# One VectorE instruction per modulation block, and a planner's time line with traced durations, in a two-part transformer forward pass

## The chip, the cores and the metric

One NeuronCore of a Trainium2 chip runs one program. The metric is the device time of one launch in microseconds (us); lower is better. All operands live in HBM before the launch and the result is written back to HBM.

## What is computed

The reference chains two small transformers over 512 tokens of width 1024, all in float32. The first has two layers, each a hybrid mixer (window attention, dense attention, spatial gating), a cross attention and a convolutional feed-forward network. The second has an even layer (a state-space mixer beside differential attention), an odd layer (retention beside sliding-window attention) and an MLP after each. Every sublayer of the second part is wrapped in a modulation that depends on one vector `c` alone:

```
c_act = jax.nn.silu(c)
...
def sandwich(x, c_act, sublayer, g_pre, g_post, w_mod, b_mod):
    shift, scale, gate = jnp.split(c_act @ w_mod + b_mod, 3, axis=-1)
    h = rms_norm_2(x, g_pre) * (1 + scale[:, None]) + shift[:, None]
    return x + gate[:, None] * rms_norm_2(sublayer(h), g_post)
```

There are four such sublayers, so `c_act @ w_mod` is four products of a vector of 1024 with a matrix of 1024 by 3072. In the kernel it is 96 blocks of 128 rows by 1024 columns: 8 blocks (one per 128 rows of `w_mod`) sum to one of 12 results.

## The kernel before

**Products.** A float32 product is made of three TensorE products of `fp32r` halves: a weight block of 128x1024 arrives by DMA as `raw`, ScalarE writes its high half `whi`, VectorE the rest `wlo` (`split_block`, line 489), and `mm3` (line 501) issues hi*hi, hi*lo and lo*hi. Activations are kept transposed as `fTh`/`fTl`. There are 531 such blocks. Names in the trace: `bank` is a PSUM tile, `W`-like names are weight halves, `gh`/`gl` the halves of a feed-forward activation.

**Order of the work.** Nothing is scheduled by the compiler. The Python program keeps a *time line* (`Line`, line 194): for every instruction that it emits, `add` works out when the engine and the operands would be free, with a duration from `cost` (line 262). Work that is to come later is put on a heap by `defer` (line 345), with a due time from that time line (when its operands are ready), and `poll` (line 332) emits what is due after every few TensorE instructions. `pump` (line 459) splits weight blocks ahead while VectorE's time on the line is at most 1 us past TensorE's. So the numbers in `cost` decide in which order each in-order engine gets its instructions; the chip waits on semaphores where reality is later than the line. Every recorded instruction has the source line 186 (the recorder).

**The modulation** is done inside the two convolutional feed-forward stages, 48 blocks in each. `mod_step` (line 1282) is called after each feature product; `mod_go` (line 1289) handles one block `mraw` once its DMA is due on the line. The first of 8 blocks is scaled into the accumulator `macc` by ScalarE; each of the other 7 is scaled in place by ScalarE and added by GpSimd (POOL). After the eighth, `sums` is deferred: four TensorE products with a matrix of ones add up the 128 rows of `macc`.

**Other places.** `hybrid` (line 871) loads the gate bias `bg` and halves it on VectorE as the first thing of a layer. `launch` (line 851) starts the 16 attention units of a branch, whose `probs_out` (line 765) writes the tiles `pt0`, `pt1`. `diff` runs eight heads that share one buffer `qkl`.

Of the kernel before, what the change touches and what calls it, by code (L numbers as in the profile page):

```python
# [13 lines left out]
F32R = mybir.dt.float32r  # L14
# [8 lines left out]
NT = S // P  # L23
# [170 lines left out]
class Line:  # L194
# [66 lines left out]
    @staticmethod  # L261
    def cost(eng, op, n, ins, outs):
        if op == "dma_start":
            return 1.03 if eng == "gpsimd" else 0.05
        if eng == "tensor":
            if op == "transpose":
                return 0.107
            fast, m = ins[0].dtype == F32R, ins[0].shape[1]
            if m > 64:
                return max(n / 2400 + 0.003, 0.108 if n > 64 else 0.2) if fast else max(n / 600 + 0.005, 0.22)  # L270
            return max(n, 64) / (2400 if fast else 600) * (0.56 if m > 32 else 0.29)
        if eng == "vector":
            if op == "tensor_scalar_mul":
                return 0.06 + n / 1530
            return (0.13 if op == "scalar_tensor_tensor" else 0.07) + n / 960
        if eng == "scalar":
            return 0.03 + n / 1120 + 0.08 * max(0, len(ins) + len(outs) - 2)
        return 0.07 + n / 460 if n > 64 else 0.62


class Block:
# [22 lines left out]
class KB:  # L304
# [460 lines left out]
    def probs_out(self, pool, u):  # L765


        nc, sh = self.nc, u.shared
        if not sh:
            sh["pt"] = [self.tile(pool, (P, u.wide // P, 2, P), f"pt{e}") for e in range(2)]  # L770
            sh["ev"] = Event(2, lambda: self.defer(0, pv, *sh["pt"]))
        for e in range(2):
            pp = self.ps((P, 4, P))
            self.transpose4(pp, [u.sc[e][:, b * P:b * P + P] for b in range(u.nkb)])
            pt = sh["pt"][e][:, :u.nkb, u.pr, :]
            if e == 0:
                nc.scalar.activation(pt, pp[:, :u.nkb, :], AF.Copy)
            else:
                nc.vector.tensor_copy(pt, pp[:, :u.nkb, :])
        u.read.set()  # L780

        def pv():
            po = self.ps((P, 2 * P))
            vc = slice(64 * u.kv, 64 * u.kv + 64)
            for b in range(u.nkb):
                for e in range(2):
                    nc.tensor.matmul(po[64 * e:64 * e + 64, :], lhsT=u.v[:, u.b0 + b, vc],
                                     rhs=sh["pt"][e][:, b, :, :].rearrange("p r q -> p (r q)"),
                                     start=b == 0, stop=b == u.nkb - 1)
            self.poll()  # L790
            sl, k = slice(u.i * P, u.i * P + P), 2 * u.kv
            self.split(u.br.h[:, k:k + 2, sl], u.br.l[:, k:k + 2, sl], po.rearrange("p (r q) -> p r q", r=2))

        sh["ev"].set()

# [55 lines left out]
    def launch(self, pool, unit, step, br, **kw):  # L851


        units, depth = [], kw["bufs"] // 2

        def start(n):
            if n >= depth and not units[n - depth].read.done:
                units[n - depth].read.after(lambda: self.defer(0, lambda: start(n)))
                return
            unit(pool, units[n])  # L860

        for n in range(16):
            kv, i, pr = n // 8, n // 2 % 4, n % 2
            u = Unit(kv=kv, i=i, pr=pr, shared={} if pr == 0 else units[-1].shared, br=br, read=Event(),
                     **{k: v for k, v in kw.items() if k != "band"})
            u.b0, u.nkb, u.add = kw["band"](i)
            units.append(u)
            self.defer(n * step, lambda n=n: start(n), kw["kh"], kw["kl"])


    def hybrid(self, l, xT):
        nc, A = self.nc, self.A
        with self.pool("hp") as hp:
            W = Weights(self, "w_in", l)
            WB = Weights(self, "w_branch", l)
            bg = self.load(hp, A["b_gate"][l], (P, 24), "bg")
            nc.vector.tensor_scalar_mul(bg, bg, 0.5)
            mg = self.tile(hp, (P, KD, S), "mg")

            def branch(n, br, first, done=None):  # L880
                wb = None
                for m in range(KD):
                    c = n * 8 + m
                    ps = self.dense(W.next(), 0, xT, KD)
                    gt = self.tile(hp, (P, S), "gt", 2)
                    nc.scalar.activation(gt, ps, AF.Tanh, bias=bg[:, c:c + 1], scale=0.5)
                    if m % 2 == 0:
                        wb = WB.next()
                    ps = self.dense(wb, (m % 2) * P, br, 4, keep=m % 2 == 0)
                    if first:  # L890
                        nc.vector.scalar_tensor_tensor(mg[:, m, :], gt, 1.0, ps, op0=ALU.add, op1=ALU.mult)
                    else:
                        nc.vector.scalar_tensor_tensor(gt, gt, 1.0, ps, op0=ALU.add, op1=ALU.mult)
                        nc.vector.tensor_tensor(mg[:, m, :], mg[:, m, :], gt, op=ALU.add)
                    if done:
                        done(m)

            def new_br():
                return FT(*self.pair(hp, (P, 4, S), "br", 2))

            brc = new_br()
            with self.pool("cp") as cp:
                self.branch_c(cp, l, xT, W, brc)
                self.flush()
            bra = new_br()
            with self.pool("ap") as ap, ExitStack() as es:
                self.branch_ab(es, ap, l, xT, W, bra, "a")
                branch(2, brc, True)
                self.flush()
            brb = new_br()  # L910
            with self.pool("ap") as ap, ExitStack() as es:
                self.branch_ab(es, ap, l, xT, W, brb, "b")
                branch(0, bra, False)
                self.flush()
            with self.pool("mt") as mt:
                hi, lo = self.pair(mt, (P, KD, S), "mT")
                mT = FT(hi, lo, (), [Event() for _ in range(KD)])

                def merged(m):
                    def go():  # L920
                        self.split(hi[:, m, :], lo[:, m, :], mg[:, m, :], scale=0.5)
                        mT.ev_k[m].set()
                    self.defer(0, go, mg[:, m, :])

                branch(1, brb, False, merged)
                self.flush_to_k(mT)
                self.open_boundary(self.open_right(), A["ln1_g"], A["ln1_b"], l)
                WM = Weights(self, "w_mix_out", l)
                fT, after = self.ln_start()
                self.tok(WM, mT, KD, 512, lambda t, ps: self.residual(t, 0, ps), by_k=True)  # L930
                self.tok(WM, mT, KD, 512, lambda t, ps: (self.residual(t, 1, ps), after(t)))
        return fT
# [356 lines left out]
    def mod_go(self):  # L1289
# [9 lines left out]
        if k == 0:  # L1299
            self.mod_acc = self.tile(self.mod_pool, (P, D), "macc", 2)  # L1300
            nc.scalar.activation(self.mod_acc, raw, AF.Copy, scale=ck)
        else:
            nc.scalar.activation(raw, raw, AF.Copy, scale=ck)
            nc.gpsimd.tensor_tensor(self.mod_acc, self.mod_acc, raw, op=ALU.add)
        if k == KD - 1:
            acc, row = self.mod_acc, self.mod_sums[kind][s]

# [428 lines left out]
    def diff(self, dp, hT, W, v, yT):  # L1736
        nc, A = self.nc, self.A
        sub = self.load(dp, A["e_diff_norm"], (P, 1), "sub")
        nc.vector.tensor_scalar_mul(sub, sub, 1.0 - LAM_INIT)

        def head(h):
            T = self.tile(dp, (P, 512), "T", 2)
            self.toeplitz(T, h, 0, 512)
            qk = []
            shared = {}

            def unit(i):
# [3 lines left out]
                for m in range(2):  # L1751
                    ps = self.ps()
                    self.scores(ps[:, :Wd], qk[0][:, m, i * P:i * P + P], qk[1][:, m, :Wd], qk[2][:, m, :Wd], Wd)
                    s = self.tile(dp, (P, Wd), f"sc{i}", 2)
                    nc.vector.tensor_tensor_reduce(s, ps[:, :Wd], T[:, 384 - i * P:512], 1.0, NEG,
                                                   ALU.add, ALU.max, mx[:, m:m + 1])
                    s2.append(s)
                nc.vector.tensor_scalar_mul(nm_, mx, -1.0)
                for m in range(2):
                    nc.scalar.activation(s2[m], s2[m], AF.Exp, bias=nm_[:, m:m + 1], accum_out=sums[:, m:m + 1])  # L1760
# [49 lines left out]
            def ev(i, ps):  # L1810
                t = self.tile(dp, (P, 2, S), f"qk{i}", 2, F32R)
                qk.append(t)
                if i == 0:
                    self.stack_q([t[:, e, :] for e in range(2)], ps, HD ** -0.5)
                else:
                    qk.append(self.tile(dp, (P, 2, S), "qkl", 1, F32R))
                    self.stack_k(t, qk[2], ps)
                    for n in range(NT):
# [295 lines left out]
```

## Time and profile before

| | |
|---|---|
| median of 3 runs | 3478.86 us (3476.7 to 3480.21) |
| the profiled execution's own time | 3478.01 us |
| its span, first to last instruction | 3476.2 us |
| mean granted TensorE clock | 0.987 |
| busy: TensorE / VectorE / ScalarE / GpSimd | 3366.9 / 2078.5 / 1433.7 / 347.3 us |

The span is 1.8 us less than the execution's own time. A busy time is the sum of the stretches in which an engine had an instruction in it. Where TensorE is not busy, a view of waits names the engine whose result it waited for.

### The profile page before, as it was taken

To read this page: it belongs to the slowest core of one execution; us is meant where nothing else is said; L and a number is where in the kernel's file an instruction comes from. 1 tells how busy PE (TensorE), PEld (TensorE's weight loads), DVE (VectorE), ACT (ScalarE), POOL (GpSimd) and SP (SyncE) were. 2 spreads that over 40 slices of the span, in tenths; PEclk is the share of its full clock that TensorE was granted. 3 is DMA by queue.
4 is the path that set the end of the run, shared out by engine and by line. 5 is a ranking of instruction groups with operands and counts; after the bars stand their busy time and mean duration, and the time that the engine had idled before them with its cause. 6 is when DMAs were issued, how large, how long until landed. Compare 5 with 4: busy or idle time off the path is not lost. (4 is left out here: it accounts for less than half of the span.)

```text
span 3476.2 us, 42309 instructions
## 1 busy us (share of the span) xinstructions
PE 3366.9 (97%) x16500; PEld 2749.0 (79%) x16500; DVE 2078.5 (60%) x3370; ACT 1433.7 (41%) x2497; POOL 347.3 (10%) x250
## 2 busy tenths in 40 slices
PE   8999999999999999999999899999999999999999
PEld 6887887777778878887777678777888887888887
DVE  5767467665667674676656666487433466553334
ACT  3544334544335452444543343475332344433222
POOL 0010001432200100013322000001000010010000
PEclk9999999999999999999999999999999999999999
DMA  4221445644332224445443221313322331333222
GB/s 147 70 69 60 143 155 181 207 164 145 118 118 70 72 67 140 158 177 182 162 153 118 86 79 55 100 49 136 104 97 97 121 111 55 103 138 109 93 95 87
DMA packets 116760, 399.24 MB, mean 115 GB/s; under 512 B 14608, under 2 KB 18592, under 8 KB 116560
## 3 DMA queue, kind: packets, MB, share of 16 engines
q1 hardware_dynamic: 115984, 394.44, 33.4%
q8 instruction: 130, 2.13, 0.2%
q0 software_dynamic: 576, 2.10, 0.2%
q14 instruction: 70, 0.57, 0.1%
HBM read 375.39 MB, written 23.71 MB: 115 GB/s over the span
## 5 line engine op out<-in xcount | busy, mean ns | idle before, releaser
L186 DVE TENSOR_TENSOR wlo<-raw,whi 128x1024 fp32r<-128x1024 f32 x531 | 716.5, 1354 | 688.5 <-ACT whi L186 678.4
L186 PE MATMUL bank<-fTh,whi 128*128 128x512 f32 (+1 forms) x2320 | 886.8, 382 | 0.0
L186 PE MATMUL bank<-fTl,whi 128*128 128x512 f32 (+1 forms) x2320 | 872.4, 376 | 0.4
L186 PE MATMUL bank<-fTh,wlo 128*128 128x512 f32 (+1 forms) x2320 | 871.8, 376 | 0.1
L186 ACT ACTIVATE whi<-raw 128x1024 fp32r<-128x1024 f32 x531 | 553.6, 1047 | 379.2 <-PE bank L186 345.8
L186 PEld LDWEIGHTS bank<-fTh,whi 128*128 128x128 f32 x2320 | 441.4, 190 | 90.5 <-issue 10.5
L186 PEld LDWEIGHTS bank<-fTh,wlo 128*128 128x128 f32 x2320 | 441.0, 190 | 85.4 <-DVE wlo L186 0.5
L186 PEld LDWEIGHTS bank<-fTl,whi 128*128 128x128 f32 x2320 | 441.5, 190 | 79.8 <-DVE fTl L186 1.3
L186 PE MATMUL bank<-whi,gh 128*128 128x512 f32 x864 | 343.2, 397 | 0.0
L186 PE MATMUL bank<-whi,gl 128*128 128x512 f32 x864 | 342.5, 396 | 0.0
L186 PE MATMUL bank<-wlo,gh 128*128 128x512 f32 x864 | 342.4, 396 | 0.0
L186 POOL TENSOR_TENSOR macc<-macc,mraw 128x1024 f32<-128x1024 f32 x84 | 225.9, 2690 | 449.2 <-ACT mraw L186 448.0
L186 PE MATMUL bank<-whi,fTh 128*128 128x512 f32 (+2 forms) x608 | 231.5, 381 | 12.8 <-ACT whi L186 7.1
L186 PE MATMUL bank<-wlo,fTh 128*128 128x512 f32 (+2 forms) x608 | 224.1, 369 | 9.9 <-DVE wlo L186 9.9
L186 PE MATMUL bank<-whi,fTl 128*128 128x512 f32 (+2 forms) x608 | 223.7, 368 | 0.5 <-DVE fTl L186 0.5
L186 PEld LDWEIGHTS bank<-whi,gh 128*128 128x128 f32 x864 | 163.1, 189 | 40.1 <-issue 0.8
L186 PEld LDWEIGHTS bank<-wlo,gh 128*128 128x128 f32 x864 | 163.2, 189 | 39.4
L186 PEld LDWEIGHTS bank<-whi,gl 128*128 128x128 f32 x864 | 162.9, 188 | 39.5
L186 POOL TENSOR_TENSOR rstd<-rstdv,mhalf 128x1 f32<-128x1 f32 x68 | 56.5, 832 | 1053.1 <-DVE rstdv L186 1050.5
L186 DVE SCALAR_TENSOR_TENSOR y<-bank,cv,y 128x511 f32<-128x511 f32 x176 | 131.3, 747 | 37.2 <-ACT y L186 34.1
L186 PEld LDWEIGHTS bank<-whi,fTh 128*128 128x128 f32 x608 | 115.9, 191 | 33.7 <-ACT whi L186 8.8
L186 PEld LDWEIGHTS bank<-wlo,fTh 128*128 128x128 f32 x608 | 116.0, 191 | 29.7 <-DVE wlo L186 12.3
(322 smaller groups left out, 4649.4 us busy)
## 6 DMA issues: line engine op xcount, KB each, us to landing
raw<-in_mlp_w_dram SPq DMA_DIRECT2D x128, 512.0 KB, 3.3
mraw<-in_mod_w_dram SPq DMA_DIRECT2D x96, 512.0 KB, 4.7
raw<-in_w_in_dram SPq DMA_DIRECT2D x88, 512.0 KB, 3.3
raw<-in_f_w_up_dram SPq DMA_DIRECT2D x88, 512.0 KB, 4.2
raw<-in_e_w_in_dram SPq DMA_DIRECT2D x48, 512.0 KB, 4.1
raw<-in_f_w_down_dram SPq DMA_DIRECT2D x40, 512.0 KB, 3.5
raw<-in_o_w_in_dram SPq DMA_DIRECT2D x30, 512.0 KB, 4.3
raw<-in_w_branch_dram SPq DMA_DIRECT2D x24, 512.0 KB, 3.3
```

Of the source, the lines that this page charges most:

```text
L186: r = f(*a, **k)
```

## The change

Three things change. The seven additions per result become one `scalar_tensor_tensor` on VectorE each (`macc = mraw * ck + macc`), which replaces both the ScalarE scaling and the GpSimd addition. The durations in `cost` get other constants. And three ordering details are new: an attention unit's `probs_out` waits until the products of the pair of units before it have been emitted, a `diff` head writes its key halves only after the scores of the head before, and the halving of `bg` stands behind branch c.

```diff
@@ cost
-            fast, m = ins[0].dtype == F32R, ins[0].shape[1]
+            m = ins[0].shape[1]
+            if ins[0].dtype == F32R:
+                return max(n / 2270 + 0.007, 0.112)
             if m > 64:
-                return max(n / 2400 + 0.003, 0.108 if n > 64 else 0.2) if fast else max(n / 600 + 0.005, 0.22)
-            return max(n, 64) / (2400 if fast else 600) * (0.56 if m > 32 else 0.29)
+                return max(n / 600 + 0.005, 0.22)
+            return max(n, 64) / 600 * (0.56 if m > 32 else 0.29)
         if eng == "vector":
             if op == "tensor_scalar_mul":
-                return 0.06 + n / 1530
-            return (0.13 if op == "scalar_tensor_tensor" else 0.07) + n / 960
+                return 0.15 + n / 1530
+            return (0.21 if op == "scalar_tensor_tensor" else 0.155) + n / 960
         if eng == "scalar":
-            return 0.03 + n / 1120 + 0.08 * max(0, len(ins) + len(outs) - 2)
-        return 0.07 + n / 460 if n > 64 else 0.62
+            acc = len(outs) > 1
+            return 0.145 + n / 1128 + (0.19 if acc else 0.0) + 0.09 * max(0, len(ins) + len(outs) - 2 - acc)
+        return 0.07 + n / 460 if n > 64 else 0.6
@@ probs_out
+        if not u.before.done:
+            u.before.after(lambda: self.defer(0, lambda: self.probs_out(pool, u)))
+            return
...
             self.split(u.br.h[:, k:k + 2, sl], u.br.l[:, k:k + 2, sl], po.rearrange("p (r q) -> p r q", r=2))
+            u.over.set()
@@ launch
+            u.before, u.over = (units[-1].before, units[-1].over) if pr else (units[-1].over if units else Event(0), Event())
@@ hybrid
-            nc.vector.tensor_scalar_mul(bg, bg, 0.5)
...
                 self.branch_c(cp, l, xT, W, brc)
+                nc.vector.tensor_scalar_mul(bg, bg, 0.5)
@@ mod_go
-            nc.scalar.activation(raw, raw, AF.Copy, scale=ck)
-            nc.gpsimd.tensor_tensor(self.mod_acc, self.mod_acc, raw, op=ALU.add)
+            nc.vector.scalar_tensor_tensor(self.mod_acc, raw, ck, self.mod_acc, op0=ALU.mult, op1=ALU.add)
@@ diff
+        scored = [Event(0)]
         def head(h):
+            before, now = scored[-1], Event(NT)
+            scored.append(now)
...
+                now.set()
...
+                    self.wait(before)
                     qk.append(self.tile(dp, (P, 2, S), "qkl", 1, F32R))
```

The new constants reorder all engines. Two places matter below. First, VectorE at the start of the program, from the memset of `ones` on (`fTl` is the low half of the transposed input, `bg` the gate bias). Before:

```order
L186 MEMSET ones 128x128
L186 TENSOR_SCALAR bg_114<-bg_114 128x24
L186 TENSOR_TENSOR fTl_93<-bank_25_133,fTh_92 128x4x128
L186 TENSOR_TENSOR fTl_93<-bank_26_140,fTh_92 128x4x128
L186 TENSOR_TENSOR wlo_148<-raw_99,whi_147 128x1024
L186 TENSOR_TENSOR fTl_93<-bank_30_156,fTh_92 128x4x128
```

Now:

```order
L186 MEMSET ones 128x128
L186 TENSOR_TENSOR fTl_93<-bank_25_132,fTh_92 128x4x128
L186 TENSOR_TENSOR fTl_93<-bank_26_139,fTh_92 128x4x128
L186 TENSOR_TENSOR wlo_147<-raw_99,whi_146 128x1024
L186 TENSOR_TENSOR fTl_93<-bank_30_155,fTh_92 128x4x128
L186 TENSOR_TENSOR fTl_93<-bank_31_162,fTh_92 128x4x128
```

The row that reads `bg` no longer stands ahead of the first input halves; it comes after branch c.

Second, TensorE around the second sum of the modulation in the first feed-forward stage (`macc` with `ones`). Before:

```order
L186 MATMUL bank_1159_5890<-fTh_4854,whi_5746 128x512
L186 MATMUL bank_1159_5890<-fTl_4855,whi_5746 128x512
L186 MATMUL bank_1159_5890<-fTh_4854,wlo_5747 128x512
L186 MATMUL bank_1165_5922<-macc_5632,ones 32x256 x4
L186 MATMUL bank_1159_5890<-fTh_4854,whi_5746 128x512
```

Now:

```order
L186 MATMUL bank_1159_5900<-whi_5855,gh_5362 128x512
L186 MATMUL bank_1159_5900<-wlo_5856,gh_5362 128x512
L186 MATMUL bank_1159_5900<-whi_5855,gl_5363 128x512
L186 MATMUL bank_1164_5917<-macc_5616,ones 32x256 x4
L186 MATMUL bank_1160_5901<-whi_5855,gh_5362 128x512
```

The sum has moved from within the last feature product of the group to nine products behind its end. On VectorE the last addition of that sum now stands here, between two splits and the two convolution steps of the last feature product:

```order
L186 TENSOR_TENSOR wlo_5856<-raw_5725,whi_5855 128x1024
L186 SCALAR_TENSOR_TENSOR macc_5616<-mraw_5791,cact,macc_5616 128x1024
L186 SCALAR_TENSOR_TENSOR y_1156_5894<-bank_1152_5861,cv_5075,y_1156_5894 128x511 x2
L186 TENSOR_TENSOR wlo_5903<-raw_5776,whi_5902 128x1024
L186 TENSOR_TENSOR y_1156_5894<-y_1148_5850,y_1156_5894 128x512
```

The two convolution steps behind the addition read the bank of the last feature product, so the addition stands ahead of work that needs that product's end, and the sum on TensorE behind it.

## Rows read from the trace of the kernel before

**Rows 1.** The page: busy time of each engine, share of the span, instructions

```profile
PE 3366.9 (97%) x16500; PEld 2749.0 (79%) x16500; DVE 2078.5 (60%) x3370; ACT 1433.7 (41%) x2497; POOL 347.3 (10%) x250
```

**Rows 2.** TensorE's waits: releaser, us in total, times, longest

```profile
PE bank L186 <- POOL macc L186: 36.5, 12, 5.1
PE bank L186 <- DVE ss L186: 14.1, 3, 4.8
PE bank L186 <- DVE wlo L186: 9.9, 5, 6.1
PE bank L186 <- ACT whi L186: 7.1, 4, 2.5
...
PE bank L186 <- ACT fTh L186: 5.7, 1, 5.7
...
PE bank L186 <- DVE mx L186: 3.5, 2, 1.9
PE bank L186 <- ACT bank L186: 2.9, 4, 1.3
```

**Rows 3.** Timeline, second sum: start, us, engine, instruction, idle before and releaser

```profile
653.60 2.68 DVE L186 TENSOR_TENSOR wlo<-raw,whi 128x1024 fp32r<-128x1024 f32 x1 [2.75 <-ACT whi L186]
...
660.81 1.13 ACT L186 ACTIVATE mraw<-mraw,cact 128x1024 f32<-128x1024 f32 x1
...
662.09 2.35 POOL L186 TENSOR_TENSOR macc<-macc,mraw 128x1024 f32<-128x1024 f32 x1 [3.53 <-ACT mraw L186]
...
664.49 1.08 PE L186 MATMUL bank<-macc,ones 128*32 128x256 f32 x8 [5.08 <-POOL macc L186]
```

**Rows 4.** Stretches: busy us of PE, PEld, DVE, ACT, POOL; granted clock; DMA

```profile
661.00:664.49 3.49, 0.01 (x1) 0.01 (x1) 2.13 (x3) 1.83 (x3) 2.35 (x1) 0.60 0.82 305
664.49:668.30 3.81, 3.81 (x15) 2.43 (x16) 1.38 (x2) 3.78 (x6) 0.00 (x0) 0.50 0.60 209
...
667.00:668.00 1.00, 1.00 (x4) 0.81 (x3) 1.00 (x1) 0.97 (x3) 0.00 (x0) 0.50 0.11 41
...
669.00:670.00 1.00, 1.00 (x6) 0.77 (x6) 0.60 (x2) 1.00 (x2) 0.92 (x1) 1.00 0.77 209
```

**Rows 5.** Same view: both feed-forward stages, and 50 us of uninterrupted products

```profile
569.00:905.00 336.00, 317.62 (x1434) 254.81 (x1435) 213.44 (x196) 161.38 (x194) 113.09 (x42) 0.97 0.52 179
1517.00:1853.00 336.00, 317.45 (x1431) 255.22 (x1432) 211.54 (x194) 160.84 (x193) 112.85 (x42) 0.97 0.49 172
...
2550.00:2600.00 50.00, 50.00 (x216) 40.25 (x215) 20.24 (x23) 15.13 (x19) 0.00 (x0) 1.00 0.29 97
```

**Rows 6.** Groups by form, 569 to 905 us: busy, mean ns, idle before

```profile
L186 DVE TENSOR_TENSOR wlo<-raw,whi 128x1024 fp32r<-128x1024 f32 x56 | 105.5, 1887 | 68.5 <-ACT whi L186 65.1 <-DMA mraw<-in_mod_w_dram 3.0
L186 DVE TENSOR_TENSOR y<-y,y 128x512 f32<-128x512 f32 x19 | 24.0, 1263 | 0.0
...
L186 ACT ACTIVATE mraw<-mraw,cact 128x1024 f32<-128x1024 f32 x42 | 47.5, 1138 | 0.0
...
L186 POOL TENSOR_TENSOR macc<-macc,mraw 128x1024 f32<-128x1024 f32 x42 | 113.1, 2693 | 224.5 <-ACT mraw L186 223.9
```

**Rows 7.** Groups by form: splits in 50 to 470 us, others in the span

```profile
L186 DVE TENSOR_TENSOR wlo<-raw,whi 128x1024 fp32r<-128x1024 f32 x59 | 71.8, 1222 | 55.0 <-ACT whi L186 52.9 <-PE bank L186 1.8 <-DMA gb<-in_ln_b_dram 0.3
...
L186 DVE TENSOR_TENSOR r<-r 128x512 f32<-128x512 f32 x64 | 43.8, 684 | 0.0
...
L186 DVE SCALAR_TENSOR_TENSOR y<-y,rstd,gb 128x1024 f32<-128x1024 f32 x20 | 25.7, 1285 | 3.8 <-POOL rstd L186 2.2
```

**Rows 8.** Timeline of the first 25 us: ScalarE, VectorE and TensorE

```profile
8.02 1.05 ACT L186 ACTIVATE whi<-raw 128x1024 fp32r<-128x1024 f32 x1
9.12 0.80 PE L186 MATMUL bank<-whi,fTh 128*128 128x512 f32 x1 [1.63 <-ACT whi L186]
13.44 0.18 DVE L186 TENSOR_SCALAR bg<-bg 128x24 f32<-128x24 f32 x1 [10.32 <-DMA bg<-in_b_gate_dram]
16.00 0.80 PE L186 MATMUL bank<-wlo,fTh 128*128 128x512 f32 x1 [6.08 <-DVE wlo L186]
```

## Prediction

> **What bounds the kernel now.** I begin with the table of busy times: TensorE is busy for 97% of the span, 3366.9 us, with VectorE at 60% [rows 1]. So the time is TensorE's products, plus its idle time of 3476.2 - 3366.9 = 109.3 us, plus what a lower granted clock adds to the products. The change gives TensorE neither more nor fewer products, so it can only act on the idle time and the clock.
>
> The view of TensorE's waits says who owns the idle time. The largest entry, 36.5 us in 12 times, is `macc`: the sum of the modulation waits for GpSimd's last addition, once for each of the 12 results [rows 2]. The other entries that this change can reach are smaller: `ss` 14.1, `wlo` 9.9, `whi` 7.1, `fTh` 5.7, `mx` 3.5, `bank` 2.9.
>
> The timeline shows how one such wait comes about [rows 3]. ScalarE scales the last `mraw` by 661.94, GpSimd begins its addition at 662.09 after standing idle for 3.53 us, takes 2.35 us, and the sum on TensorE starts at 664.49 after 5.08 us of idleness. TensorE is in order, so the feature products behind the sum wait with it, though they need nothing of it. GpSimd is not full, as its idle time before that addition says. The line that orders the queues believes in a shorter chain (by the old constants 0.944 us for the scaling and 2.296 for the addition; their rows have 1.138 and 2.693 [rows 6]) and puts the sum too early.
>
> The stretches show a second cost behind the wait [rows 4]. In the idle stretch the granted clock falls to 0.60 on the mean, and in the 3.81 us after it TensorE is fully busy at 0.50, the 1.2 GHz level: 4 products fit in a microsecond, against 6 once the clock is at 1.00 again, the 2.4 GHz level. These products take twice their time, so some 3.8 / 2 = 1.9 us are lost, and they are booked as busy, not as waiting. The same view for each whole feed-forward stage gives a granted clock of 0.97 over 336 us, that is 10 us below full in each, 20 us in both, part of it inside the idle time; a piece of plain products elsewhere runs at 1.00 [rows 5].
>
> **The change part by part.** The profiled execution took 3478.01 us, 0.85 us less than the median of the runs, and I count from it.
>
> *Term A, the addition.* Removed: 84 scalings on ScalarE at 1.138 us (95.6 us) and 84 additions on GpSimd at 2.693 us (226 us) [rows 6]. Added: 84 `scalar_tensor_tensor` on VectorE. A row of the same form, operation and size is `y<-y,rstd,gb` at 1.285 us [rows 7], so 84 x 1.285 = 108 us, 54 in each stage. I bound one of them by the 684 ns of a half-sized operation [rows 7] and by 1.887 us, the mean of a split in this stage [rows 6].
>
> VectorE gets room for it. In the first feed-forward stage it is busy 213.44 of 336 us [rows 5], and its operations with two SBUF operands are slow there: a split's `wlo` takes 1887 ns on the mean against 1222 ns in the span's quieter part, `y<-y,y` 1263 against 684 for a two-operand form of its size [rows 6, 7]. The timeline has one such split of 2.68 us [rows 3]. GpSimd's additions are the one thing this stage has and the others don't. If they are the cause, 56 x 0.665 = 37 us and 19 x 0.579 = 11 us go away in the stage, 48 in all, against 54 added: VectorE stays near 219 of 336 us. If they are not the cause, it comes to 267 of 336. Either is below the stage's length.
>
> The sum no longer waits for a chain of three engines. In the new order the last addition of the second sum stands ahead of two convolution steps that read the bank of the last feature product, and the sum on TensorE stands nine products behind that product. Those nine take about 9 x 0.23 = 2.1 us (50 us hold 216 products [rows 5]), and the addition itself cannot be behind work that TensorE has yet to begin. I therefore take all 36.5 us of the waits as gone, and with them the half-clock stretches. Eight of the twelve waits lie between 3.2 and 5.1 us; the other four are under 0.9. Eight times 1.9 is 15 us; I bound this by 8 us and by the whole 20 of the stages' clock. Sum of the term: 36.5 + 15 = **-52 us**, bounds -44 and -56.
>
> ScalarE's scalings and GpSimd's additions give nothing further: both engines are below half of their stage [rows 5], so their time only counts through `macc` and through VectorE's splits. `mraw` now comes free after one instruction instead of two, so the loads of the next blocks start no later; their number on SP's queue is the same.
>
> *Term B, `bg` at the start.* VectorE stands idle for 10.32 us behind the DMA of `bg`, until 13.44 us, with the low halves and the first `wlo` behind it. TensorE has its first `whi` at 9.12 us and then waits 6.08 us for `wlo`, until 16.00 [rows 8]. Without `bg` ahead, `wlo` can follow `whi`, which ends at 9.07, by about 10.3 us, so the second product could start 5.6 us earlier. Cover for the loss is the input itself: of the 16.00 us part is spent loading `x`, and later tiles may stand in the same queue as `bg`. I take -5 us, with bounds 0 (the input was to be waited for in any case) and -7.7 (both waits of [rows 8] go). Moved behind branch c, the 0.18 us instruction [rows 8] lies beside hundreds of products, and its data has long landed.
>
> *Term C, the new order elsewhere.* The gate on `probs_out` and the wait in `diff` hold back ScalarE's and VectorE's work, and the new constants move splits and evictions on all engines. What they can win is in the small entries: `mx` 3.5, `bank` 2.9 and, after the start, some 7.5 us of `whi` and `wlo` [rows 2], 14 us in all. They can also add as much, where `probs_out` or the key halves become the late thing; the wait in `diff` has the next head's scores queued behind it. Nothing in the trace measures this. The new constants are nearer to the rows than the old (a 1024-wide two-operand VectorE instruction was taken as 1.137 us, is now 1.222, and takes 1222 ns [rows 7]), which speaks for a small gain: -4 us, bounds -14 and +14.
>
> The waits for `ss` (14.1) and `fTh` (5.7) [rows 2] hang on chains of normalisation at the borders of layers, in which every step needs the one before. An order cannot shorten them; I leave them.
>
> Sum: 3478.0 - 52 - 5 - 4 = 3417, and with the 0.85 us to the median **3418 us**, 1.7% less than before. The bounds added at their ends give 3478.0 - 56 - 7.7 - 14 = 3400 and 3478.0 - 44 - 0 + 14 = 3448.
>
> **The rivals.**
>
> *Half of the waits stay: 3443 us.* VectorE is in order too. If the line places the sum as tightly as before, each last addition stands behind a split or a convolution step of 1.2 us [rows 7], and TensorE waits two to three microseconds instead of three to five. Then half of term A remains: 3478 - 26 - 9 = 3443. For it speaks that VectorE works on both the weights and `macc`, while GpSimd had little else to do. Against it: the nine products between, and that the duration used for the addition (1.277 us by the new constants) is that of the row, where GpSimd's was too short by 0.4 us.
>
> *VectorE becomes what TensorE waits for: 3525 us, slower.* The place is the split of a weight block in the feed-forward stages. Suppose that `wlo` stays at 1887 ns and each of the 84 additions delays a split which TensorE is just about to need; then TensorE pays the addition in full, 84 x 1.285 = 108 us, and the gain is used up: 3478 - 52 - 9 + 108 = 3525. It decides from 61 / 84 = 0.73 us of new waiting for each addition on. For it: the 68.5 us in which VectorE idles ahead of `wlo` are ScalarE's doing [rows 6], so its spare time isn't all usable. Against it: 267 of 336 us even in that case, no wait for `wlo` inside these stages worth naming now, and splits that `pump` makes ahead.
>
> The Trainium skill, "Perfetto Trace Analysis", section "Optimizing Scalar/DVE Operations", says that a saturated VectorE should shed work to ScalarE or even GPSIMD, which speaks against this change, and adds that GPSIMD and VectorE share a read port of SBUF, so that moving work between these two might not help. By its first half the outcome would be this rival's; by the rows, in which VectorE has 36% of the stage free and is slowest beside GpSimd, it is the forecast.
>
> *The sum was only the first thing to be late: 3474 us.* TensorE does not stop for `macc` any more, but reaches the end of the stage earlier and waits there, for the convolution steps, for weights in transit, or for the next border; the DMA share in the stage is 0.52 [rows 5], so the weights could be the one. Then only part of term B is left, 3478 - 4 = 3474, and the change does not do what it says. Against it: that share leaves the DMA half of its time, and no wait for `raw` stands among TensorE's larger ones [rows 2].
>
> **How the numbers follow.** The forecast has a chance of 0.77, half of the waits staying 0.12, VectorE in the way 0.06, the moved wait 0.05. The range 3400 to 3448 holds the forecast with its bounds and most of the second case; about 2 in 10 are left for the rest. About 0.2%, 7 us, is what a measurement of this kernel can tell from no change. Faster by more than that come the forecast and the half case, 0.89; the moved wait is the case within it, 0.05; slower is VectorE's, 0.06.
>
> **What would show it right or wrong.** Right: TensorE's waits hold no entry for GpSimd's `macc`, and one for VectorE's `macc` of a few microseconds at most; the feed-forward stages shrink by some 26 us each and run at a granted clock of 0.99 or more; `wlo` and `y<-y,y` fall to about 1.22 and 0.7 us there; VectorE stays near 65% of them; the second product starts near 10.4 us. Wrong: an entry for VectorE's `macc` of 15 us or more (the half case); `wlo` at 1.9 us still, with waits for it grown in the feed-forward stages (VectorE in the way); stages shorter, but as much new waiting for `ss`, `x` or `raw` (the moved wait); or new entries for `pt`, `mx` or `qkl` in the attention parts beyond 14 us, by which term C would be wrong.

## The result and the profile after

The changed kernel takes 3434.76 us (median of 4 runs, 3431.74 to 3435.64) against 3477.78 us for the kernel before beside it: a ratio of 0.9875, with a 95% interval of 0.9858 to 0.9892. That is 43 us less where the sum of the terms was 61, and inside the range. The profiled execution took 3431.74 us with a span of 3429.9, that is 46.3 us shorter than the span before.

Busy times (the page, as in [rows 1]):

```profile
PE 3349.7 (98%) x16500; PEld 2736.8 (80%) x16500; DVE 2079.8 (61%) x3454; ACT 1353.1 (39%) x2411; POOL 122.8 (4%) x166
```

TensorE's idle time fell from 109.3 to 80.2 us, and its busy time by 17.2 us with the same 16500 products: the granted clock, whose mean went from 0.987 to 0.993, makes the same products shorter. VectorE took 84 more instructions and is busy for 1.3 us more.

TensorE's waits after the change (releaser, us, times, longest):

```profile
PE bank L186 <- DVE ss L186: 13.1, 3, 4.9
PE bank L186 <- DVE y L186: 12.4, 9, 1.6
PE bank L186 <- DVE wlo L186: 10.3, 15, 2.1
PE bank L186 <- ACT whi L186: 8.8, 5, 4.0
PE bank L186 <- DMA x<-in_x_dram: 5.0, 1, 5.0
PE bank L186 <- ACT fTh L186: 4.8, 1, 4.8
PE bank L186 <- DMA mem<-in_mem_dram: 3.6, 2, 1.9
...
PE bank L186 <- ACT oTh L186: 2.7, 4, 0.7
```

Beside [rows 2] the entry for `macc` is gone, all 36.5 us. That of `wlo` hides two movements: the 6.08 us at the start [rows 8] went, and small waits came in many places. `y` doubled, and `mem` and `oTh` came up; before, these three were

```profile
PE bank L186 <- DVE y L186: 6.1, 8, 1.7
...
PE bank L186 <- ACT oTh L186: 1.4, 2, 0.7
...
PE bank L186 <- DMA mem<-in_mem_dram: 0.3, 2, 0.2
```

The two feed-forward stages (us, busy of TensorE, weight load, VectorE, ScalarE, GpSimd; clock, DMA), cut so that each begins at its first transposes and ends at the place of [rows 5]:

```profile
567.60:879.60 312.00, 311.04 (x1430) 249.44 (x1431) 214.15 (x239) 119.29 (x151) 0.00 (x0) 1.00 0.56 192
1497.30:1807.00 309.70, 309.35 (x1426) 249.46 (x1427) 213.66 (x237) 118.82 (x150) 0.00 (x0) 1.00 0.53 185
```

They are 312.0 and 309.7 us long, about 24 and 26 less than the 336 before; TensorE idles 1.0 and 0.4 us in them, at a clock of 1.00. VectorE's operations in the first (groups by form, as in [rows 6]):

```profile
L186 DVE TENSOR_TENSOR wlo<-raw,whi 128x1024 fp32r<-128x1024 f32 x55 | 67.0, 1224 | 41.3 <-ACT whi L186 38.6 <-DMA ms<-msum 2.6
L186 DVE SCALAR_TENSOR_TENSOR y<-bank,cv,y 128x511 f32<-128x511 f32 x80 | 59.9, 749 | 19.4 <-ACT y L186 18.0
L186 DVE SCALAR_TENSOR_TENSOR macc<-mraw,cact,macc 128x1024 f32<-128x1024 f32 x42 | 53.7, 1278 | 0.2
...
L186 DVE TENSOR_TENSOR y<-y,y 128x512 f32<-128x512 f32 x19 | 13.0, 684 | 0.0
```

Splits fell from 1887 to 1224 ns and `y<-y,y` from 1263 to 684, so the 53.7 us of additions were paid, nearly in full, by the time that the other operations no longer lost, and VectorE's load stayed (213 us before, 214 after). The convolution steps that read a PSUM bank, 747 ns before, are 749 now.

The second sum (timeline of VectorE, then of TensorE, as in [rows 3]):

```profile
654.94 1.23 DVE L186 TENSOR_TENSOR wlo<-raw,whi 128x1024 fp32r<-128x1024 f32 x1 [1.71 <-ACT whi L186]
656.08 1.28 DVE L186 SCALAR_TENSOR_TENSOR macc<-mraw,cact,macc 128x1024 f32<-128x1024 f32 x1
```

```profile
657.95 0.40 PE L186 MATMUL bank<-whi,gl 128*128 128x512 f32 x1
658.28 0.64 PE L186 MATMUL bank<-macc,ones 128*32 128x256 f32 x8
658.85 0.50 PE L186 MATMUL bank<-whi,gh 128*128 128x512 f32 x1
```

The last addition ends at 657.36 us; the sum starts at 658.28 with nothing to wait for.

### The profile page after: what moved, and what is told of

The parts are those of the page before. It is cut to its first block, busy times and chain, and to the rows that moved or that the text cites. A ratio compares the mean times of both kernels' runs of the same rounds, so it can differ in the third digit from the quotient of the medians.

```text
span 3429.9 us, 42045 instructions
## 1 busy us (share of the span) xinstructions
PE 3349.7 (98%) x16500; PEld 2736.8 (80%) x16500; DVE 2079.8 (61%) x3454; ACT 1353.1 (39%) x2411; POOL 122.8 (4%) x166
## 5 line engine op out<-in xcount | busy, mean ns | idle before, releaser
L186 DVE TENSOR_TENSOR wlo<-raw,whi 128x1024 fp32r<-128x1024 f32 x531 | 641.3, 1214 | 622.9 <-ACT whi L186 613.1
L186 DVE TENSOR_TENSOR y<-y,bank 128x512 f32<-128x512 f32 x96 | 65.0, 684 | 113.3 <-PE bank L186 113.1
L186 PEld LDWEIGHTS bank<-whi,fTl 128*128 128x128 f32 x608 | 115.8, 190 | 20.9 <-DVE fTl L186 1.2
```

The lines of the kernel that those rows point to most:

```text
L186: r = f(*a, **k)
```

## The experiments

Each ratio is to the kernel before on the same chip, with its 95% interval; the change has 0.9875. A difference of some 0.002 between two of them is not told apart.

**1. The addition alone.** The kernel before, with the two lines of `mod_go` replaced:

```diff
-            nc.scalar.activation(raw, raw, AF.Copy, scale=ck)
-            nc.gpsimd.tensor_tensor(self.mod_acc, self.mod_acc, raw, op=ALU.add)
+            nc.vector.scalar_tensor_tensor(self.mod_acc, raw, ck, self.mod_acc, op0=ALU.mult, op1=ALU.add)
```

> The kernel before with one edit: the seven additions per result are one VectorE instruction each; constants, gates and the place of the bg halving stay those of before. Theory (the feed-forward stages' 50 us come from the chain ScalarE and GpSimd itself, so the engine change alone brings them): 3478 - 50 = 3428 us, no wait for macc of GpSimd, wlo near 1.22 us in the first feed-forward stage, first wait for wlo still at 16 us; since the new order elsewhere cost 9 us in the change, this would be some 7 us faster than the change. Rival (the sum is placed right only by the new constants): about half of the macc waits stay, now for VectorE, 3450 to 3455 us.

Measured: 3426.19 us, 0.9865 (0.9852 to 0.9879). There is no `macc` entry, and the others are close to those of before, the start included (the largest differences are `whi`, 9.1 us for 7.1, and `mem`, 1.7 for 0.3):

```profile
PE bank L186 <- DVE ss L186: 14.2, 3, 4.9
PE bank L186 <- DVE wlo L186: 9.9, 5, 6.1
...
PE bank L186 <- DVE y L186: 7.2, 9, 1.7
```

This edit alone brings what the whole change brings; the 7 us that I expected it to be ahead of the change don't show, as the two ratios can't be told apart. It does so although its constants take the addition as 1.197 us where its rows have 1.277.

**2. The pair kept.** The change with that edit taken back.

> The change with its modulation put back to the ScalarE scaling and the GpSimd addition; new constants, gates and late bg halving stay. Theory (the gain is the engine change): macc waits of 30 us or more come back with the half-clock stretches, wlo is at 1.9 us in the feed-forward stage, 3435 + 50 = 3485 us. Rival (the constants alone placed the sum late enough): macc waits under 10 us in all, clock of the stages at 0.99, 3435 to 3445 us, with wlo still at 1.9 us.

Measured: 3470.67 us, 0.999 (0.9981 to 0.9999). The first entry of the waits is

```profile
PE bank L186 <- POOL macc L186: 27.1, 11, 5.0
```

So the new constants, which lengthen ScalarE's scaling on the line by 0.11 us and a split by 0.085 and leave GpSimd's addition as it was, take 9 of the 36 us away and leave the rest: neither my "30 us or more" nor the rival's "under 10". The time came out 14 us below what I expected. These 9 us are part of that, and some 4 us are the chip, on which the kernel before takes 3474.22 us.

**3. `bg` first.** The change, with the halving back at the head of `hybrid`:

```diff
             bg = self.load(hp, A["b_gate"][l], (P, 24), "bg")
+            nc.vector.tensor_scalar_mul(bg, bg, 0.5)
...
-                nc.vector.tensor_scalar_mul(bg, bg, 0.5)
```

> The change with the halving of bg back at the head of the layer. Theory (term B, VectorE is in order and stood behind the bg transfer): the second product starts near 16 us again, some 5 us slower than the change, 3440 us. Rival (the start is bound by the x and weight transfers, or the loss is made good by the mixer): 3435 us.

Measured: 3439.29 us, 0.9903 (0.989 to 0.9917), against 0.9875. VectorE and TensorE at the start:

```profile
13.06 0.18 DVE L186 TENSOR_SCALAR bg<-bg 128x24 f32<-128x24 f32 x1 [9.95 <-DMA bg<-in_b_gate_dram]
```

```profile
15.62 0.79 PE L186 MATMUL bank<-wlo,fTh 128*128 128x512 f32 x1 [5.90 <-DVE wlo L186]
```

In the change that product stands at

```profile
9.79 0.80 PE L186 MATMUL bank<-wlo,fTh 128*128 128x512 f32 x1 [0.46 <-DVE wlo L186]
```

The difference of the ratios, 0.0028 of 3478, is 10 us; by the intervals it may be as little as the 5 expected or none. The two profiled spans differ by 6.3 us.

**4. The old constants.** The change with all of `cost` as before (the gates, the VectorE addition and the late `bg` stay).

> The change with the constants of before; VectorE addition, gates and late bg halving stay. Theory (the 9 us that the mixers, the cross attentions and the second part lost come from the order that the new constants make): 3435 - 9 = 3426 us, perhaps less, with the wait for mem near 0.3 us and the waits for wlo after the start near 3 us. Rival 1 (the loss is the gates'): 3433 to 3436. Rival 2 (the new constants were needed to place the sums): over 3440, with waits for macc.

Measured: 3421.72 us, 0.9851 (0.9838 to 0.9865), and in the waits

```profile
PE bank L186 <- DVE y L186: 7.2, 9, 1.7
PE bank L186 <- DVE wlo L186: 5.0, 9, 0.8
...
PE bank L186 <- DMA mem<-in_mem_dram: 0.3, 1, 0.3
```

The loss elsewhere belongs to the constants; the sums don't need them. By the ratios alone the step from 0.9875 to 0.9851 is at the limit of what can be told apart; it is the three entries, back at their sizes of before or near them, that show it. Run 4 differs from run 1 by the gates and the late `bg` alone, and its ratio by 0.0014, 5 us, no more than the start is worth (`wlo` falls from 9.9 us to 5.0). So the gates show neither a gain nor a cost of their own.

**5. The sum later.** The kernel before with one line changed: ScalarE and GpSimd still make `macc`, but the sum is due 6 us after its last addition.

```diff
-            self.defer(0, sums, acc)
+            self.defer(0.0 if self.planning else max(0.0, nc.ready(acc) - self.now()) + 6.0, sums)
```

> The kernel before with one edit: the sum of each result is deferred until 6 us after its last addition is done on the line; ScalarE scaling and GpSimd addition, old constants and everything else stay. Theory (the price is a sum that stands too early in TensorE's in-order queue, whichever engine adds): the 36 us of macc waits and the half-clock stretches go, 3474 - 50 = 3424 us, although wlo stays at 1.9 us in the feed-forward stages. Rival (GpSimd's additions also cost through the slowed splits): waits for wlo or y appear in the feed-forward stages once the macc waits no longer give VectorE its pauses, 3435 to 3450 us.

Measured: 3429.71 us, 0.9871 (0.9858 to 0.9885): the gain of the whole change, without the instruction it is named for. `macc` keeps 5.3 us in 2 waits. Splits are still slow in the first feed-forward stage, and TensorE waits for none of them:

```profile
L186 DVE TENSOR_TENSOR wlo<-raw,whi 128x1024 fp32r<-128x1024 f32 x57 | 106.8, 1878 | 59.4 <-ACT whi L186 58.5 <-DMA ms<-msum 0.5
```

```profile
PE bank L186 <- POOL macc L186: 3.6, 1, 3.6
PE bank L186 <- DVE y L186: 1.7, 1, 1.7
```

(The second fence is the whole list of TensorE's waits from 568 to 900 us.) The price before was the place of the sum in TensorE's queue: with the sum later, faster splits are not needed for the gain.

**6 to 8. One engine's constants at a time.** The change with the lines of one engine in `cost` put back.

> The change with only TensorE's constants of before. If they make the loss of 10 to 13 us that all old constants took away (3431 to 3422 us on this chip): 3422 us, the entry for mem near 0.3 us and that for y near 7. If VectorE's or ScalarE's make it: 3431 us, mem 3.6 and y 12 as in the change. My expectation is the second, since the products' constants differ least.

Measured: 3492.1 us, 1.0046 (1.0032 to 1.0059), slower than before. Both forecasts fell. The waits:

```profile
PE bank L186 <- DVE wlo L186: 34.0, 29, 4.6
PE bank L186 <- ACT whi L186: 19.7, 12, 3.8
```

With TensorE's products taken as 0.2163 us and VectorE's operations at their longer new times, the line sees VectorE further behind than it is, and TensorE waits 41 times for a half of a weight block. That the one makes the other is my reading; no run separates it.

> The change with only VectorE's constants of before (a split taken as 1.137 us instead of 1.222). If longer VectorE durations let pump split fewer blocks ahead, and so leave wlo late: the waits for wlo fall from 10.3 us in 15 to near 5 us, and the time from 3431 to 3424 us. If not: 3431 us with wlo near 10.

Measured: 3415.0 us, 0.983 (0.9816 to 0.9843), the lowest of all, though runs 10 and 12 can't be told from it. But `wlo` stays at 10.0 us in 9 waits, so my mechanism (fewer blocks split ahead) is not what made it faster. The first entries are

```profile
PE bank L186 <- DVE y L186: 12.4, 12, 3.1
PE bank L186 <- DVE wlo L186: 10.0, 9, 2.6
PE bank L186 <- DVE ss L186: 9.2, 2, 4.6
```

`ss` fell by 3.9, `whi` by 4.2, `mem` by 3.4 and `fTh` by 4.8 us against the change, mostly chains at the borders of layers.

> The change with only ScalarE's constants of before (a 1024-wide instruction taken as 0.944 us instead of 1.053). If the loss is ScalarE's part (oTh, whi and, through the layer border, mem and y later on the line): oTh falls from 2.7 to 1.4 us, y from 12 to 7 us, and the time from 3431 to 3425 us. If not: 3431 us.

Measured: 3430.6 us, 0.9871 (0.9858 to 0.9885), as the change. `oTh` fell to 1.4 us as expected, `y` stayed at 12.4.

**9 and 10. Distance of starts, and two times.** First the change with VectorE's and ScalarE's old constants and TensorE's new ones. Then also a later time for results, in `add`:

```diff
             end = self.free["dma"] + 2.5
+        end += {"vector": 0.085, "scalar": 0.1}.get(eng, 0.0)
```

> The change with VectorE's and ScalarE's constants of before, and TensorE's of the change. In the trace of the change two 1024-wide VectorE operations that follow each other start 1.14 us apart, though each lasts 1.222; on ScalarE 0.95 against 1.05; on TensorE 512-wide products start 0.23 us apart. Theory (what the line needs is the distance of starts, how long the engine is taken up): old constants of VectorE (1.137) and ScalarE (0.944) and the new ones of TensorE (0.2326) are the right ones, 3410 to 3415 us, below the 3415 of VectorE's alone. Rival (the new constants only differ by chance of the order): anywhere from 3415 to 3435 us.

Measured: 3428.52 us, 0.9856 (0.9842 to 0.9869). The theory fell: it is slower than with VectorE's old constants alone (0.983), not faster. The time lies in the rival's span.

> As the run before, and the line keeps two times for VectorE and ScalarE: the engine is free after the distance of starts, the result is ready 0.085 us (VectorE) or 0.1 us (ScalarE) later, which is the rest of the duration. Theory (both times matter, each in its place): the few waits that a result is believed ready too early shrink, 3405 to 3412 us. Rival (the line's fixed lag already covers that rest): as the run before within 3 us.

Measured: 3420.77 us, 0.9835 (0.9822 to 0.9849). The second time brings 0.0021, and the two intervals just overlap. It comes level with the run of VectorE's old constants, no better, and misses the 3405 to 3412 us of the theory.

**11 and 12. The pair in the best order.** The kernel of 0.983 with the ScalarE and GpSimd pair put back and the sum 6, then 12 us later.

> The change with VectorE's constants of before, the ScalarE scaling and the GpSimd addition put back, and each sum deferred until 6 us after its last addition. Theory (only the place of the sum mattered, the engine that adds does not): within 4 us of the same kernel with the VectorE addition, 3413 to 3419 us, with wlo at 1.88 us in the feed-forward stages. Rival (the slowed splits cost once the order is better): 3425 us or more, with waits for wlo in these stages.

Measured: 3428.01 us, 0.985 (0.9837 to 0.9864), with 8.5 us of `macc` in two waits. That is outside the 3413 to 3419 us of the theory, though as a ratio it can't be told from 0.983. A split takes 1.83 us on the mean in the first feed-forward stage, and TensorE waits for none of them there, so the rival's reason is not what is seen.

> The run with the pair kept, VectorE's constants of before and the later sum, now 12 us after the last addition instead of 6, since two waits for macc of 8.5 us in all were left there. Theory (only the sum's place matters): these waits go, and the ratio to the kernel before falls from 0.985 to that of the same kernel with the VectorE addition, 0.983, with wlo still at 1.8 us or more in the feed-forward stages. Rival (the splits slowed beside GpSimd's additions are worth something in the better order): the ratio stays at 0.985 or above, without macc waits.

Measured: 3422.61 us, 0.9837 (0.9824 to 0.9851). No `macc` wait is left, as the theory has it, and a split takes 1.89 us in the first feed-forward stage; the first entry of the waits is

```profile
PE bank L186 <- DVE wlo L186: 13.5, 10, 2.6
```

That is 3.5 us more than with the VectorE addition. Two of these waits stand where the down products begin, where the other kernel has 0.3 us:

```profile
655.30 0.50 PE L186 MATMUL bank<-wlo,gh 128*128 128x512 f32 x1 [1.85 <-DVE wlo L186]
...
1583.92 0.79 PE L186 MATMUL bank<-wlo,gh 128*128 128x512 f32 x1 [2.14 <-DVE wlo L186]
```

So here slow splits do make TensorE wait: the engine that adds is worth a few microseconds, which the times can't tell apart.

## Why the prediction was right, and which term was wrong

The spans of the two profiled executions, cut at the same instructions:

| term | forecast | trace |
|---|---|---|
| A, both feed-forward stages | -52 | -24 and -26 |
| B, start | -5 | -5 (first gate evaluation of `gt`, 112.6 to 107.5 us) |
| C, order elsewhere | -4 | +9 (46.3 in all, less the others) |

*Term A* held in size, and by both of its mechanisms. In the two stages TensorE's idle time fell from 36.9 to 1.3 us and its busy time by 14.7 us, the part of the clock, which is at 1.00 now (forecast 36.5 and 15). One reason given for it was too narrow. I put it down to the shorter chain of engines. Run 5 shows that the chain may stay if the sum stands later; run 2 shows that the new constants without either still leave 27 us of it.

The prediction was also short on why the line put the sum too early. It names the durations of the scaling and of the addition. In the wait that it shows [rows 3], these are 0.19 and 0.05 us above the line's figures, of 5.08 us. The rows ahead of them in the kernel before show more:

```profile
652.76 2.43 POOL L186 TENSOR_TENSOR macc<-macc,mraw 128x1024 f32<-128x1024 f32 x1 [6.50 <-ACT mraw L186]
...
655.42 3.13 POOL L186 TENSOR_TENSOR macc<-macc,mraw 128x1024 f32<-128x1024 f32 x1 [0.23 <-ACT mraw L186]
...
656.20 1.52 DVE L186 SCALAR_TENSOR_TENSOR y<-bank,cv,y 128x511 f32<-128x511 f32 x2
...
657.64 2.00 DVE L186 TENSOR_TENSOR wlo<-raw,whi 128x1024 fp32r<-128x1024 f32 x1
...
659.56 0.68 DVE L186 TENSOR_TENSOR y<-y,y 128x512 f32<-128x512 f32 x1
...
660.28 0.63 ACT L186 ACTIVATE gh<-y 128x512 fp32r<-128x512 f32 x1 [4.05 <-DVE y L186]
...
666.92 1.22 DVE L186 TENSOR_TENSOR wlo<-raw,whi 128x1024 fp32r<-128x1024 f32 x1 [2.74 <-ACT whi L186]
```

ScalarE comes to the last scaling (660.81) only after `gh<-y`, for which it stood idle for 4.05 us until VectorE had `y`. VectorE had been busy without a pause since 653.60, and in that time it did two splits of 2.68 and 2.00 us, which the line takes as 1.137 each. So the splits slowed beside GpSimd's own additions made the last addition late, by some 2.4 us here (my estimate from these rows). With the addition on VectorE both go, the chain and the slow splits; no run parts the two. The rest of the 5.08 us I have not traced.

The shorter times of VectorE's other operations came as worked out, and they pay for the addition.

*Term B* held: -5, with the second product at 9.79 us where I worked out 10.4.

*Term C* is the term that was mis-sized, and it had the wrong sign: +9 for -4, inside its bounds of 14. The step that failed reads: "The new constants are nearer to the rows than the old ..., which speaks for a small gain". Run 4 shows the contrary: with the constants of before the loss is gone. Its place is the mixers and cross attentions of the two layers. The lead of the change falls from 5.0 us at 110 us to 1.5 at the first feed-forward stage, and from 25.4 us at the end of that stage to 20.0 at the second; in these stretches TensorE waits 7.0 and 10.3 us where it waited 3.8 and 6.3 before. In the second part the waits moved about, and the lead is 46.1 us at its start and 46.3 at its end.

A second sentence of the prediction fell with the runs: that an order cannot shorten the waits for `ss` and `fTh`. In the change they are nearly as before, but run 7, which differs from it only in VectorE's constants, has `ss` at 9.2 us for 14.1 before and no entry for `fTh`.

A duration is not the time that an engine is taken up. Three splits that follow one another in the changed kernel are one row:

```profile
37.67 3.49 DVE L186 TENSOR_TENSOR wlo<-raw,whi 128x1024 fp32r<-128x1024 f32 x3
```

3.49 less one duration of 1.222 leaves 2.27 for two starts, 1.13 us each. The old constant (1.137) was the distance of starts; the new one (1.222) is the duration, and counts 0.09 us too many for each such operation when VectorE is in a run of them. The Trainium skill, "Perfetto Trace Analysis", section "DVE / Act Engine Instruction (TENSOR_ADD, Activation, etc)", says that the reported window ends when the write is acknowledged, and that the next instruction may begin its prefetch before that, when the execution is over. The trace agrees, with 1.13 us between starts for 1.222 of duration.

Runs 7, 9 and 10 show that this is not the whole of it. VectorE's old constants alone gain most (0.983), VectorE's and ScalarE's together less (0.9856), and with a separate time for results the ratio is 0.9835 again. So these runs don't show that either kind of time is the right one for the line; the rival of run 9, that the differences are chance of the order, stands. Why ScalarE's old constants cost 9 us beside VectorE's old ones (run 7 to run 9) and nothing beside the new ones (0.9875 to 0.9871, run 8) stays open.

*The rivals.* Half of the waits staying did not happen, and neither did VectorE become the bound: it is busy 214 of 312 us in the first of these stages, where TensorE waits 0.7 us for its splits:

```profile
PE bank L186 <- DVE wlo L186: 0.7, 2, 0.5
```

Nor did the wait move on to the end of these stages. The gain is 18 us smaller than forecast: 2 in term A, 13 in term C, and 3 us by which the profiled execution lies below the median of its runs.

## What to carry to other kernels

If an in-order engine waits long for a small result that others behind it don't need, try first to place the reader later: here one line was worth as much as moving the work to another engine (0.9871 and 0.9865). Where a planner orders the work, treat any change of its numbers as a new order that has to be timed: constants whose values for a product of 512 columns, a split and a 1024-wide ScalarE operation differ by 7 to 12% moved this kernel between 0.983 and 1.005. Constants nearer to the trace did not make it faster by themselves, and giving the line both the distance of starts and the whole duration (run 10) came level with the best and did not beat it.

## What the runs showed of the hardware

A GpSimd addition with both operands in SBUF slows VectorE's operations with two SBUF operands: on the mean of a stage a split takes 1887 ns for 1224, and `y<-y,y` 1263 for 684. Those that read PSUM stay where they were (747 and 749). The means mix two kinds. In the first stage before, of the 48 splits that the timeline lists one by one, the 16 with no addition beside them take 1.21 to 1.23 us, four of them beside a scaling of ScalarE, and the 32 with one take 1.92 to 3.03. It looks like waiting and not like slower work: the first split of the rows above begins inside an addition that ends at 655.19 and ends at 656.28, and the second begins inside one that ends at 658.55 and ends at 659.64, each 1.09 us behind the addition, whatever it had taken by then. The other splits that outlast an addition in which they began do the same, within 0.02 us.

That such slow splits, 37 us of them in a stage, cost nothing once the sum stands later (run 5) I had not expected; run 12 shows the limit, with two waits of 1.85 and 2.14 us for them. Nor had I expected that the old VectorE constant, 7% under the duration, was the distance of starts.
